# A bias table stored once instead of 128 times, two norm borders with their filler products moved, and two matrix products padded with zero rows

## The chip, the core and the metric

The kernel runs on one core of one Trainium2 chip, as one launch. A core has four compute engines that matter here: TensorE (PE, matrix products, with its weight loads shown apart as PEld), VectorE (DVE), ScalarE (ACT) and GpSimd (POOL); SyncE (SP) issues the DMA transfers of this kernel, all on one queue that 16 DMA engines work off. Each engine runs its own instructions in program order and waits on semaphores for the others. The metric is the device time of one execution in microseconds (us), the median of several runs.

## What is computed

A chain of three transformer-like blocks on one sequence of 256 tokens of width 1024, in float32. Cut to what the change touches:

```
# block 1: retention + RG-LRU, gated (g_l = x_n @ w_in[gl]); rms_norm out
# block 2: attention with relative bias, conv, pooling, then two layer norms
rel  = r[:, None] - r[None, :]                      # query - key, 256 x 256
own  = q @ k.T * 64**-0.5 + tab[t5_bucket(rel)]     # tab: rel_bias, 8 heads x 32 buckets
own  = where(rel >= 0, own, -1e30)
attn = softmax(own) @ v
x = layer_norm(alpha * x + mix, ln1_g, ln1_b)       # border 1
up = causal_dwconv(x @ w_up, ffn_conv_w) + ffn_conv_b
x = layer_norm(alpha * x + (u * silu(g)) @ w_down, ln2_g, ln2_b)   # border 2
# block 3: swiglu_ffn(rms_norm(x)), rwkv7 time mix, swiglu, cross attention to a memory
#          (k, v = rms_norm(mem) @ w), gmlp
kk = kk / max(norm(kk, per head), 1e-12)            # rwkv: 16 heads of 64
g  = sigmoid(xg @ g1) @ g2                          # rwkv gate, inner width 160
```

## The kernel before

**Tiling.** Activations lie feature-major: x is [128 partitions, 8, 256 tokens]. All weights stream through SBUF as blocks of 1 MB (128 x 2048 float32). `_dma` (L434) issues one block on SP; `_split` then cuts each half of it into two parts, a rounded high half that ACT copies (L455) and the low remainder that DVE subtracts (L458). A product is three passes over those parts in PE (L543/L547 for 512 and 256 wide operands, L545 to L547, L562 to L564 for token-major output), accumulated in PSUM tiles `psd` (4 buffers) and `psx` (4 buffers).

**Order.** The order of instructions on each engine is that in which the Python code emits them. Evictions and side work are put off by `later`, `soon` and `chain`: closures that `tick` and `tock` run at each later column group. `pump` issues the next weight block and the next splits when an estimate of the DMA queue (`_queued(us)`, a clock that each transfer advances) says they fit.

**Bias table.** `bias_table` (L1205 to L1221) multiplies a one-hot bucket matrix (33 x 384, from `_buckets`) with the bias values (33 x 8): L1217 on PE, L1218 copies the 8 x 384 result out on ACT, and L1219 writes it to DRAM, each head's row 128 times (8 x 128 x 384 float32, 1.57 MB). This is emitted in block 1, between blocks of the weights `w_in_k` and `w_in_gl`. Block 2 reads it back at L1230 as a tile of 128 x 8 x 256, in which each partition starts one element earlier in its own copy of the row, and `top()` adds it to the scores (L1264, shown in the trace under L369, the helper that issues it).

**Borders.** `ln_finish` (L1081 to L1130) is the layer norm after a linear layer; it runs after the attention output (border 1, into `up`) and after `down` (border 2, into the first ffn of block 3). In it PE has the mean product (L1089, which needs the accumulated `acc` of L1079), then the variance product (L1104), and DVE the subtraction (L1093), the reciprocal root (from L374 on) and the normalised outputs (L369). Since PE would have nothing else, `fill(n)` puts n memory units there: each is 16 matmuls of the memory's keys (L543/L547) or values (L566/L567), with an eviction later (L628/L629, or at the values a scaled one, L366/L369). The argument `units` says how many stand ahead of the mean product, between it and the variance product, and behind. At border 2 the norm factor of the next rms norm follows: `rms_stats(nxt, at)` emits L721 and its DVE steps from L724 on, `at` calls of `tick` later, inside the first column group of the ffn.

**Rwkv.** L1805 multiplies the per-head factors `nt` (8 rows) with `heads` (8 rows) and L1839 the second part of the gate (32 rows of 160), both with the contraction on 8 or 32 partitions.

Of the kernel before, what the change touches and what calls it, by code (L numbers as in the profile page):

```python
# [10 lines left out]
F32 = mybir.dt.float32  # L11
# [7 lines left out]
P = 128  # L19
T = 256  # L20
# [95 lines left out]
def _buckets():  # L116

    n = np.arange(T)
    nf = np.maximum(n, 1).astype(np.float32)
    large = 16 + (np.log(nf / np.float32(16)) / np.float32(math.log(64)) * np.float32(16)).astype(np.int32)  # L120
    bucket = np.where(n < 16, n, np.minimum(large, 31))
    out = np.zeros((33, 384), np.float32)
    for i in range(384):
        rel = 255 - i
        out[bucket[rel] if rel >= 0 else 32, i] = 1.0
    return out

# [174 lines left out]
class Net:  # L302
# [775 lines left out]
        elif m > 1:  # L1078
            self.nc.vector.tensor_add(st["acc"], st["acc"], xm)  # L1079

    def ln_finish(self, st, gname, bname, nxt=None, units=(1, 2, 3)):  # L1081

        nc, x = self.nc, self.x
        if nxt is None:
            xp = Pair(self, KD)
        self.keep = 2
        late = self.fill(units[0])
        ps = self.psum("x")
        nc.tensor.matmul(ps[:, :T], self.mean, st["acc"], start=True, stop=True)  # L1089
        sq = {}  # L1090
        for k in range(KD + 2):
            if k < KD:
                nc.vector.tensor_sub(x[:, k], x[:, k], ps[:, :T])  # L1093
                sq[k] = self.tmp("t")
                self.act(sq[k], x[:, k], AF.Square)
            if k > 2 and k % 2:
                self.stt(sq[k - 3], sq[k - 3], 1e-5 * 2 * D / P / KD, sq[k - 2], ALU.add, ALU.add)
        late += self.fill(units[1])
        self.pump()
        self.pump()  # L1100
        self._rest()
        ps = self.psum("x")
        for k in range(0, KD, 2):
            nc.tensor.matmul(ps[:, :T], self.mean, sq[k], start=k == 0, stop=k == KD - 2)  # L1104
        for f in late:
            f()
        r = self.tmp("rB", bufs=2)
        self.rsqrt(r, ps[:, :T], self.tmp("na", bufs=1))
        late = self.fill(units[2])
        ts = {}  # L1110
        for k in range(KD + 1):
            if k < KD:
                t = ts[k] = self.tmp("t")
                self.stt(t, x[:, k], self.col(gname, k), r, ALU.mult, ALU.mult)
                self.act(x[:, k], t, bias=self.col(bname, k))
                if nxt is None:
                    self.act(xp.hi(k), t, bias=self.col(bname, k))
                else:
                    self.rms_feed(nxt, k, x[:, k])
            if k and nxt is None:  # L1120
                self.stt(xp.lo(k - 1), ts[k - 1], self.col(bname, k - 1), xp.hi(k - 1).bitcast(F32), ALU.add, ALU.subtract)
            elif k:
                self.tick()
            if k == 3:
                for f in late:
                    f()
        self.drain()
        if nxt is None:
            return xp
        self.rms_stats(nxt, at=1)  # L1130

    def mem_start(self):

# [72 lines left out]
    def bias_table(self):  # L1206

        nc, io = self.nc, self.io
        oh = self.tmp("e", 512, bufs=4)[:33, :392]
        nc.sync.dma_start(oh[:, :384], io["bucket"])  # L1210
        nc.sync.dma_start(oh[:, 384:], io["relb"])
        row = self.tmp("e", 512, bufs=4)[:8, :384]
        self.bias_dram = self.pd.tile([8, P, 384], F32, name="bias_dram", tag="bias_dram")

        def run():
            ps = self.psum("x")
            nc.tensor.matmul(ps[:8, :384], oh[:, 384:], oh[:, :384], start=True, stop=True)  # L1217
            nc.scalar.copy(row, ps[:8, :384])  # L1218
            nc.sync.dma_start(self.bias_dram, row[:, None].to_broadcast([8, P, 384]))  # L1219
            self._queued(4.4)  # L1220
        self.later(6, run)  # L1221

    def block2(self, st):

        nc, io, x = self.nc, self.io, self.x
        mul, add = ALU.mult, ALU.add
        xp, r = st["xp"], st["r"]
        bias = self.slot([P, 8, T])
        b = self.bias_dram
        nc.sync.dma_start(bias, bass.AP(tensor=b.tensor, offset=b.offset + 127, ap=[[383, P], [P * 384, 8], [1, T]]))  # L1230
        misc = self.slot([P, 7 * T + 2 * P])
        pool = misc[:, 5 * T:]
        nc.sync.dma_start(pool, io["pool"])
# [12 lines left out]
        v, at = vat[:, :2], vat[:, 2:]  # L1246
# [7 lines left out]
        def soft(h):  # L1254
            s = slice(64 * (h % 2), 64 * (h % 2) + 64)
            ps = self.psum("x")
            nc.tensor.matmul(ps[:, :P], q[s, h // 2, :P], k_[s, h // 2, :P], start=True, stop=True)
            nc.tensor.matmul(ps[:, P:384], q[s, h // 2, P:], k_[s, h // 2], start=True, stop=True)
            e = es[:, h % 5]
            parts = ((0, slice(0, P)), (1, slice(P, 384)))  # L1260

            def top():
                for t, s in parts:
                    self.stt(e[:, s], ps[:, s], 0.125, bias[:, h, P - t * P:], mul, add)  # L1264
                    nc.vector.tensor_reduce(mx[:, h, t:t + 1], e[:, s], AX.X, ALU.max)
                self.ts(mx[:, h], mx[:, h], -1.0)

            def expo():
                for t, s in parts:
                    self.act(e[:, s], e[:, s], AF.Exp, bias=mx[:, h, t:t + 1], accum_out=S[:, h, t:t + 1])  # L1270
            self.soon(top)
            self.chain(expo, lambda: turn(h, e))

        def turn(h, e):
            nc.vector.reciprocal(S[:, h], S[:, h])
            pt = self.psum("x")
            for a in range(3):
                nc.tensor.transpose(pt[:, a * P:(a + 1) * P], e[:, a * P:(a + 1) * P], self.ident)
            self.soon(lambda: nc.scalar.copy(e[:, :384], pt[:, :384]))
            self.later(1 + max(0, 2 - h), lambda: attend(h, e))  # L1280
# [85 lines left out]
        st = {"acc": self.tmp("acc", bufs=2)}  # L1366
# [30 lines left out]
        st = {"acc": self.tmp("acc", bufs=2)}  # L1397
# [4 lines left out]
        nxt = self.rms_start("ffn1_norm_3", want="cols")  # L1402
# [210 lines left out]
    def rwkv(self, st, nxt):  # L1613
# [5 lines left out]
        nc, io, x, r = self.nc, self.io, self.x, st["r"]  # L1619
        mm, mul, add = nc.tensor.matmul, ALU.mult, ALU.add  # L1620
# [3 lines left out]
        self.done()  # L1624
        cst = self.slot([P, 1218 + 2 * T])
        nc.sync.dma_start(cst[:, :1218], io["rwc"])
        nt = cst[:8, 1218:].rearrange("p (f t) -> p f t", f=2)
        sel, reset = cst[:, :2], cst[:, 2:258]
        lev = cst[:, 258:386].rearrange("p (b c) -> p b c", b=4)
        nlev1, id32 = cst[:, 386:418], cst[:, 418:450]  # L1630
        gmask = cst[:, 450:706].rearrange("p (e c) -> p e c", e=2)
        heads = cst[:8, 706:1218].rearrange("p (j c) -> p j c", j=4)
        wl = [self.slot([P, WB]) for _ in range(3)]
        for t, n in zip(wl, ("lora1", "lora2", "lora3")):
            nc.sync.dma_start(t[:, :io[n].shape[1]], io[n])
        h, dx = self.slot([P, KD, T]), self.slot([P, KD, T])
# [69 lines left out]
        psl, sums = [], []  # L1706
        lt = wl[2][:, :576].rearrange("p (s c) -> p s c", s=2)
        tw = wl[2][:, 1280:].rearrange("p (n t) -> p n t", n=3)

        def lora(k):  # L1710
            if k == 0:
                psl.extend(self.psum("x") for _ in range(2))
            for n, (t, w, c) in enumerate(zip(ts.pop(k), (c1[:, k, :64], c1[:, k, 64:], g1[:, k]), (0, 64, P))):
                for s in range(2):
                    mm(psl[s][:, c:c + w.shape[1]], t[:, s * P:(s + 1) * P], w, start=k == n == 0, stop=k == 7,
                       skip_group_check=True)
            if k == 7:
                squash()
# [52 lines left out]
        def turn_norms(f):  # L1771
            ps = self.psum("x")
            for s in range(2):
                nc.tensor.transpose(ps[:8, s * P:(s + 1) * P], nn[:, 1, s, 8 * f:8 * f + 8], self.ident)
            self.soon(lambda: nc.scalar.copy(nt[:, f], ps[:8, :T]))
        self.later(5, lambda: norms(0), post=True)
        self.later(9, lambda: norms(1), post=True)

# [54 lines left out]
        def gates(m):  # L1833

            ps = self.psum("x")
            for i in range(2):
                s, o = slice((m + i) * P, (m + i + 1) * P), ps[:, i * T:(i + 1) * T]
                mm(o, wl[1][:, s], tw[:, 1], start=True, stop=False)
                mm(o, wl[1][:32, 1024 + (m + i) * P:1024 + (m + i + 1) * P], tw[:32, 2], start=False, stop=True)  # L1839
            nc.scalar.copy(flat(g[:, m:m + 2]), ps)  # L1840


# [288 lines left out]
        for m in range(0, 8, 2):  # L2131
            gates(m)
# [157 lines left out]
```

## Time and profile before

| what | value |
|---|---|
| three runs | 1838.8, 1840.44, 1840.64 us, median 1840.44 |
| the profiled execution's own time | 1836.93 us |
| its span | 1835.0 us |
| PE busy | 1784.6 us, 97% of the span |
| DVE busy | 1257.4 us, 69% |
| ACT busy | 914.0 us, 50% |
| POOL busy | 13.2 us, 1% |
| mean granted TensorE clock | 0.987 |
| DMA, mean over the span | 170 GB/s, 311.90 MB |

The span runs from the first to the last instruction that the profiler shows; 1.93 us of the execution lie around it. The profiled execution was 3.5 us shorter than the median of the runs. A granted clock of 1.00 is TensorE's upper level (2.4 GHz) and 0.50 its lower one (1.2 GHz); a stretch with both shows a value between.

### The profile page before, as it was taken

To read this page: it belongs to the slowest core of one execution; us is meant where nothing else is said; L and a number is where in the kernel's file an instruction comes from. 1 tells how busy PE (TensorE), PEld (TensorE's weight loads), DVE (VectorE), ACT (ScalarE), POOL (GpSimd) and SP (SyncE) were. 2 spreads that over 40 slices of the span, in tenths; PEclk is the share of its full clock that TensorE was granted. 3 is DMA by queue.
4 is the path that set the end of the run, shared out by engine and by line. 5 is a ranking of instruction groups with operands and counts; after the bars stand their busy time and mean duration, and the time that the engine had idled before them with its cause. 6 is when DMAs were issued, how large, how long until landed. Compare 5 with 4: busy or idle time off the path is not lost.

```text
span 1835.0 us, 27642 instructions
## 1 busy us (share of the span) xinstructions
PE 1784.6 (97%) x11142; PEld 1555.9 (85%) x11142; DVE 1257.4 (69%) x2300; ACT 914.0 (50%) x1550; POOL 13.2 (1%) x31
## 2 busy tenths in 40 slices
PE   9969999999998999999989999999999999999997
PEld 8859889899987888888589888888888899888886
DVE  7858777898757655578677675556556578676553
ACT  7738646476535544253224454444444555454441
POOL 0000000000000000001000000000000000000000
PEclk9979999999999999999989999999999999999999
DMA  8455544454563545532324354455445635445450
GB/s 312 142 147 207 186 168 167 155 188 178 186 214 130 200 171 203 184 120 78 98 103 187 135 207 172 149 201 213 162 159 207 250 118 210 159 169 194 163 184 23
DMA packets 56511, 311.90 MB, mean 170 GB/s; under 512 B 13727, under 2 KB 17856, under 8 KB 20160
## 3 DMA queue, kind: packets, MB, share of 16 engines
q1 hardware_dynamic: 56384, 310.15, 46.8%
q8 instruction: 87, 1.43, 0.3%
q14 instruction: 40, 0.33, 0.1%
HBM read 304.36 MB, written 5.77 MB: 169 GB/s over the span
## 4 chain that ended last, share of the span: by engine, by line
PE 89%; DVE 5%; DMA 3%; ACT 2%; issue 1%; SPq 0%; DVEq 0%; ACTq 0%
PE psd L543 17%; PE psd L547 14%; PE psd L562 10%; PE psd L564 10%; PE psd L563 10%; PE psd L545 5%; PE psd L546 5%; DMA s<-w_in_gl 2%; PE psx L543 2%; PE psd L2168 1%; PE psd L557 1%; DVE s L458 1%; PE psd L540 1%; PE psx L1452 1%; PE psx L547 1%
## 5 line engine op out<-in xcount | busy, mean ns | idle before, releaser
L458 DVE TENSOR_TENSOR s<-s,s 128x1024 fp32r<-128x1024 f32 x524 | 627.3, 1221 | 198.2 <-ACT s L455 197.7
L547 PE MATMUL psd<-s,s 128*128 128x256 f32 x2336 | 658.9, 282 | 3.0 <-DVE s L458 2.8
L455 ACT CAST s<-s 128x1024 fp32r<-128x1024 f32 x524 | 532.4, 1046 | 201.7 <-PE psd L547 100.6
L543 PE MATMUL psd<-s,s 128*128 128x512 f32 x1392 | 495.2, 399 | 0.0
L547 PEld LDWEIGHTS psd<-s,s 128*128 128x128 f32 x2336 | 445.1, 191 | 4.9 <-DVE s L458 4.3
L562 PE MATMUL psd<-s,s 128*128 128x512 f32 x816 | 324.9, 398 | 1.9 <-DVE s L369 1.9
L564 PE MATMUL psd<-s,s 128*128 128x512 f32 x816 | 319.6, 392 | 0.0
L563 PE MATMUL psd<-s,s 128*128 128x512 f32 x816 | 319.0, 391 | 0.0
L543 PEld LDWEIGHTS psd<-s,s 128*128 128x128 f32 x1392 | 262.1, 188 | 63.3
L545 PE MATMUL psd<-s,s 128*128 128x256 f32 x944 | 272.8, 289 | 18.6 <-DVE s L960 18.2
L546 PE MATMUL psd<-s,s 128*128 128x256 f32 x944 | 268.0, 284 | 0.0
L545 PEld LDWEIGHTS psd<-s,s 128*128 128x128 f32 x944 | 181.9, 193 | 20.5 <-DVE s L960 18.4
L546 PEld LDWEIGHTS psd<-s,s 128*128 128x128 f32 x944 | 182.0, 193 | 0.1
L562 PEld LDWEIGHTS psd<-s,s 128*128 128x128 f32 x816 | 153.9, 189 | 33.2 <-DVE s L369 2.3
L564 PEld LDWEIGHTS psd<-s,s 128*128 128x128 f32 x816 | 153.9, 189 | 33.1
L563 PEld LDWEIGHTS psd<-s,s 128*128 128x128 f32 x816 | 154.1, 189 | 30.6
L1456 DVE TENSOR_TENSOR s<-psx,s 128x512 fp32r<-128x512 f32 x44 | 30.4, 692 | 95.5 <-ACT s L1458 80.0
L366 ACT ACTIVATE t<-psd,rc 128x256 f32<-128x256 f32 x88 | 41.6, 475 | 103.5 <-PE psd L564 103.3
L1458 ACT CAST s<-psx 128x512 fp32r<-128x512 f32 x40 | 23.5, 587 | 122.4 <-PE psx L1452 122.4
L369 DVE SCALAR_TENSOR_TENSOR t<-psd,rc,t 128x256 f32<-128x256 f32 x88 | 41.5, 482 | 47.5 <-ACT t L366 47.5
L366 ACT ACTIVATE t<-x 128x256 f32<-128x256 f32 x86 | 34.1, 407 | 66.8 <-DVE x L369 45.5
L366 ACT ACTIVATE s<-x,vecs 128x256 fp32r<-128x256 f32 (+1 forms) x80 | 40.2, 506 | 50.0 <-DVE x L1416 36.4
(380 smaller groups left out, 1846.3 us busy)
## 6 DMA issues: line engine op xcount, KB each, us to landing
s<-w_ffn_in SPq DMA_DIRECT2D x88, 1024.0 KB, 4.8
s<-w_ffn_out SPq DMA_DIRECT2D x44, 1024.0 KB, 4.8
s<-w_up SPq DMA_DIRECT2D x22, 1024.0 KB, 4.9
s<-w_out SPq DMA_DIRECT2D x12, 1024.0 KB, 4.9
s<-w_down SPq DMA_DIRECT2D x11, 1024.0 KB, 4.7
s<-w_xq SPq DMA_DIRECT2D x8, 1024.0 KB, 4.8
s<-w_xo SPq DMA_DIRECT2D x8, 1024.0 KB, 4.9
s<-w_gm_v SPq DMA_DIRECT2D x8, 1024.0 KB, 4.8
```

The costliest lines, as they stand in the source:

```text
L366: return self.nc.scalar.activation(out, in_, func, **kw)
L369: return self.nc.vector.scalar_tensor_tensor(out, in0, scalar, in1, op0=op0, op1=op1)
L455: self.nc.scalar.copy(hi, raw[:, s])
L458: self.nc.vector.tensor_sub(lo, raw[:, s], hi.bitcast(F32))
L543: mm(out, w[0], x.two(k), start=first, stop=False)
L545: mm(out[:, :T], w[0], x.hi(k), start=first, stop=False)
L546: mm(out[:, :T], w[0], x.lo(k), start=False, stop=False)
L547: mm(out[:, :T], w[1], x.hi(k), start=False, stop=last)
L562: mm(out, hi, w[0], start=first, stop=False)
L563: mm(out, hi, w[1], start=False, stop=False)
L564: mm(out, lo, w[0], start=False, stop=last)
L1456: rest = lambda: nc.vector.tensor_sub(lo, both, hi.bitcast(F32))
```

## The change

Three edits that don't touch one another.

- The table in DRAM is 8 x 384, written once (12 KB instead of 1.57 MB), and the estimate of the queue no longer advances for it. `_buckets` runs the other way, and the read at L1230 takes, for partition p, 256 elements from offset p + 1 of each row, in ascending order; `top()` walks them backwards (`[::-1]`).
- `ln_finish` has `units=(2, 2, 2)` instead of `(1, 2, 3)`, and `rms_stats` is called with `at=3` instead of 1.
- In the rwkv part `nt` and `heads` use all 128 partitions and the gate product L1839 too; POOL sets `nt` (128 x 512) and a third of `tw` (128 x 256) to zero first, two MEMSETs more.

```
 _buckets:
-        rel = 255 - i
+        rel = i - P
 ln_finish:
-    def ln_finish(self, st, gname, bname, nxt=None, units=(1, 2, 3)):
+    def ln_finish(self, st, gname, bname, nxt=None, units=(2, 2, 2)):
-        self.rms_stats(nxt, at=1)
+        self.rms_stats(nxt, at=3)
 bias_table:
-        self.bias_dram = self.pd.tile([8, P, 384], F32, name="bias_dram", tag="bias_dram")
+        self.bias_dram = self.pd.tile([8, 384], F32, name="bias_dram", tag="bias_dram")
-            nc.sync.dma_start(self.bias_dram, row[:, None].to_broadcast([8, P, 384]))
-            self._queued(4.4)
+            nc.sync.dma_start(self.bias_dram, row)
 block2:
-        nc.sync.dma_start(bias, bass.AP(tensor=b.tensor, offset=b.offset + 127, ap=[[383, P], [P * 384, 8], [1, T]]))
+        nc.sync.dma_start(bias, bass.AP(tensor=b.tensor, offset=b.offset + 1, ap=[[1, P], [384, 8], [1, T]]))
-                    self.stt(e[:, s], ps[:, s], 0.125, bias[:, h, P - t * P:], mul, add)
+                    self.stt(e[:, s], ps[:, s], 0.125, bias[:, h, :P + t * P][:, ::-1], mul, add)
 rwkv:
-        nt = cst[:8, 1218:].rearrange("p (f t) -> p f t", f=2)
+        nt = cst[:, 1218:].rearrange("p (f t) -> p f t", f=2)
-        heads = cst[:8, 706:1218].rearrange("p (j c) -> p j c", j=4)
+        heads = cst[:, 706:1218].rearrange("p (j c) -> p j c", j=4)
+        nc.gpsimd.memset(nt, 0.0)
+        nc.gpsimd.memset(tw[:, 2], 0.0)
-            self.soon(lambda: nc.scalar.copy(nt[:, f], ps[:8, :T]))
+            self.soon(lambda: nc.scalar.copy(nt[:8, f], ps[:8, :T]))
-                mm(o, wl[1][:32, 1024 + (m + i) * P:1024 + (m + i + 1) * P], tw[:32, 2], start=False, stop=True)
+                mm(o, wl[1][:, 1024 + (m + i) * P:1024 + (m + i + 1) * P], tw[:, 2], start=False, stop=True)
```

On SP the order of all transfers stays; only the size of the one row at L1219 differs. PE at border 1, before: the last pair of the one memory unit that stands ahead of the mean product L1089 (`acc_410` is the sum, `psd_` the units' PSUM tiles, `s18` and `s7` weight halves), and the first pair behind it.

```order
L543 MATMUL psd_439_3543<-s18_264_2083,s16_423_3448 128x512
L547 MATMUL psd_439_3543<-s18_264_2083,s16_423_3448 128x256
L1089 MATMUL psx_441_3561<-acc_410_3334,misc_8_104 128x256
L543 MATMUL psd_450_3591<-s7_263_2082,s11_424_3451 128x512
L547 MATMUL psd_450_3591<-s7_263_2082,s11_424_3451 128x256
```

The same place after, from the last pair of the same unit (`psd_439`) on:

```order
L543 MATMUL psd_439_3543<-s18_264_2083,s16_423_3448 128x512
L547 MATMUL psd_439_3543<-s18_264_2083,s16_423_3448 128x256
L543 MATMUL psd_441_3561<-s7_263_2082,s11_424_3451 128x512
L547 MATMUL psd_441_3561<-s7_263_2082,s11_424_3451 128x256
...
L543 MATMUL psd_441_3561<-s18_264_2083,s11_424_3451 128x512
L547 MATMUL psd_441_3561<-s18_264_2083,s11_424_3451 128x256
L1089 MATMUL psx_442_3578<-acc_410_3334,misc_8_104 128x256
L543 MATMUL psd_451_3608<-s7_263_2082,s10_427_3476 128x512
```

A second unit of 16 matmuls (`psd_441`) now stands ahead of L1089; at border 2 one unit moves in the same way, and at both borders two instead of three stand behind the variance product.

PE at border 2, before: the place of the norm factor's product L721 in the first column group of the ffn (`psd_721` and `psd_722` are the two token halves, `s17` the split activations of row block k, `s15` and `s4` weight halves).

```order
L564 MATMUL psd_722_6025<-s15_674_5759,s17_677_5785 128x512
L721 MATMUL psx_724_6040<-misc_8_104,acc_676_5784 128x1 x2
L562 MATMUL psd_721_6024<-s4_675_5777,s17_677_5785 128x512
L563 MATMUL psd_721_6024<-s4_675_5777,s17_677_5785 128x512
L564 MATMUL psd_721_6024<-s4_675_5777,s17_677_5785 128x512
```

After:

```order
L564 MATMUL psd_722_6025<-s20_695_5890,s8_678_5786 128x512
L721 MATMUL psx_727_6072<-misc_8_104,acc_676_5784 128x1 x2
L562 MATMUL psd_721_6024<-s1_696_5892,s8_678_5786 128x512
L563 MATMUL psd_721_6024<-s1_696_5892,s8_678_5786 128x512
L564 MATMUL psd_721_6024<-s1_696_5892,s8_678_5786 128x512
```

L721 has moved from behind 12 matmuls of the group (row blocks k = 0 and 1) to behind 36 (k = 0 to 5), out of 48. On DVE the steps that follow it stood behind one weight split before:

```order
L704 TENSOR_TENSOR acc_676_5784<-acc_676_5784,t_717_6014 128x256
L458 TENSOR_TENSOR s5_723_6038<-s10_680_5804,s5_723_6038 128x1024
L724 COPY rcv_719_6022<-psx_724_6040 128x2
L374 TENSOR_SCALAR rc_718_6021<-rcv_719_6022 128x2
L671 TENSOR_TENSOR rca_720_6023<-rc_718_6021 128x2
```

and stand behind three after:

```order
L704 TENSOR_TENSOR acc_676_5784<-acc_676_5784,t_717_6014 128x256
L458 TENSOR_TENSOR s5_723_6038<-s10_680_5804,s5_723_6038 128x1024
L458 TENSOR_TENSOR s3_724_6052<-s10_680_5804,s3_724_6052 128x1024
L458 TENSOR_TENSOR s12_726_6069<-s0_681_5806,s12_726_6069 128x1024
L724 COPY rcv_719_6022<-psx_727_6072 128x2
```

So two splits that were behind the norm factor are now ahead of it on DVE.

## Rows read from the trace of the kernel before

**Rows 1.** PE's waits over the whole span: waiting line, releaser, total us, times, longest.
```profile
PE psd L545 <- DVE s L960: 18.2, 1, 18.2
PE psx L1937 <- issue: 3.9, 1, 3.9
```

**Rows 2.** SP's issues around the table's write: start us, us, instruction, count.
```profile
88.08 0.83 SPq L1219 DMA_DIRECT2D bias_dram<-e  x1
89.02 19.30 SPq L434 DMA_DIRECT2D s<-w_in_gl  x3
```

**Rows 3.** Windows: us, busy of five engines (count), granted clock, DMA share, GB/s.
```profile
90.00:100.00 10.00, 10.00 (x86) 10.00 (x85) 9.38 (x18) 6.82 (x11) 0.00 (x0) 1.00 0.46 51
...
128.00:133.00 5.00, 4.91 (x23) 4.91 (x24) 4.90 (x12) 3.37 (x7) 0.00 (x0) 0.50 0.78 298
133.00:138.00 5.00, 5.00 (x40) 4.89 (x40) 4.93 (x13) 3.45 (x11) 0.00 (x0) 0.97 0.08 31
```

**Rows 4.** DMA issues by tensor: count, KB each, median us from issue to landing.
```profile
s<-w_in_gr SPq DMA_DIRECT2D x4, 1024.0 KB, 4.7
...
s<-bias_dram SPq DMA_DIRECT2D x1, 1024.0 KB, 5.5
```

**Rows 5.** ACT's timeline at the stall; brackets hold idle time before and releaser.
```profile
124.02 1.99 ACT L455 CAST s<-s 128x1024 fp32r<-128x1024 f32 x2 [20.96 <-DMA s<-w_in_gl]
```

**Rows 6.** DVE's timeline at the stall, and its first use of decay.
```profile
125.10 1.22 DVE L458 TENSOR_TENSOR s<-s,s 128x1024 fp32r<-128x1024 f32 x1 [20.28 <-ACT s L455]
...
133.05 0.41 DVE L988 TENSOR_TENSOR e<-psx,s 128x256 f32<-128x256 f32 x1
```

**Rows 7.** PE's timeline at the stall.
```profile
128.09 0.58 PE L545 MATMUL psd<-s,s 128*128 128x256 f32 x1 [18.25 <-DVE s L960]
```

**Rows 8.** PE's timeline at border 1: the mean product, and the start of up.
```profile
341.16 0.91 PE L1089 MATMUL psx<-acc,misc 128*128 128x256 f32 x2 [3.61 <-DVE acc L1079]
...
359.04 0.28 PE L545 MATMUL psx<-s,s 128*128 128x256 f32 x1
```

**Rows 9.** DVE's timeline at border 1: the evictions, and the first output's low half.
```profile
349.75 1.08 DVE L629 TENSOR_TENSOR s<-psd,s 128x256 f32<-128x256 f32 x3
...
355.95 0.49 DVE L369 SCALAR_TENSOR_TENSOR s<-t,vecs,s 128x256 fp32r<-128x256 f32 x1 [0.64 <-ACT s L366]
```

**Rows 10.** Windows at the two borders, columns as in rows 3.
```profile
551.40:556.75 5.35, 5.35 (x33) 4.67 (x32) 4.69 (x13) 4.41 (x10) 0.00 (x0) 1.00 0.44 135
577.00:580.40 3.40, 3.40 (x10) 2.66 (x10) 3.12 (x11) 2.57 (x3) 0.00 (x0) 0.51 0.10 41
341.10:345.00 3.90, 3.84 (x12) 3.24 (x13) 2.90 (x10) 2.16 (x6) 0.00 (x0) 0.56 0.18 74
```

**Rows 11.** PE's timeline at border 2, the ffn's first group.
```profile
569.55 0.51 PE L562 MATMUL psd<-s,s 128*128 128x512 f32 x1 [1.89 <-DVE s L369]
...
576.40 0.61 PE L721 MATMUL psx<-misc,acc 128*128 128x1 f32 x4 [3.16 <-DVE acc L704]
...
586.49 0.39 PE L564 MATMUL psd<-s,s 128*128 128x512 f32 x1
```

**Rows 12.** DVE's timeline at border 2: the first output's low half, the last sum.
```profile
565.14 0.48 DVE L369 SCALAR_TENSOR_TENSOR s<-x,vecs,s 128x256 fp32r<-128x256 f32 x1 [0.65 <-ACT s L366]
...
575.92 0.42 DVE L704 TENSOR_TENSOR acc<-acc,t 128x256 f32<-128x256 f32 x1
```

**Rows 13.** PE's groups in the rwkv part, by shape: count, busy us, mean ns.
```profile
L1838 PE MATMUL psx<-s,s 128*128 128x256 f32 x16 | 5.6, 431 | 0.0
...
L1839 PE MATMUL psx<-s,s 32*128 32x256 f32 x16 | 5.6, 426 | 0.0
```

**Rows 14.** SP's issue of the table's read.
```profile
227.66 0.39 SPq L1230 DMA_DIRECT2D s<-bias_dram  x1
```

**Rows 15.** DVE's first use of the table.
```profile
260.70 0.28 DVE L369 SCALAR_TENSOR_TENSOR s<-psx,s 128x128 f32<-128x128 f32 x1
```

**Rows 16.** Window behind PE's wait at L1937, columns as in rows 3.
```profile
921.80:932.00 10.20, 7.91 (x113) 7.54 (x114) 6.21 (x13) 1.12 (x3) 0.00 (x0) 0.50 0.47 173
```

## The prediction, made before the changed kernel ran

> **What bounds the kernel now.** I read the page's totals first: TensorE (PE) is busy 97% of the span, so an edit pays only where PE waits, or runs at its lower clock. PE's list of waits came next. One wait of 18.2 us leads it, then 3.9 us at L1937 [rows 1]; the mean product of border 1 (3.61 us) and the norm factor's product of border 2 (3.16 us) follow [rows 8, 11]. The three edits point at three of these four places. For each I then read the timelines around it, to see what ends the wait, and the windows, to see the granted clock. Everywhere else PE runs back to back, and work taken from other engines there is worth nothing.
>
> The long wait has a simple cause. PE waits for VectorE (DVE), which waits 20.28 us for a cast on ScalarE (ACT), which waits 20.96 us for the first block of `w_in_gl` [rows 5 to 7]. That block was issued at 89.02, right behind the table's write at 88.08 [rows 2], and was there at 124.02: 35.0 us, where the same kind of block otherwise takes 4.7 [rows 4]. Between 90 and 100 us the queue moved only 51 GB/s with 0.46 of the engines' time [rows 3]. The write's 1.57 MB at that rate take 31 us, which covers 88 to 119; the block behind it needs the rest.
>
> **The table's write.** Removed: 1.57 MB on the queue. Added: 12 KB in its place, in the same order. The first block, issued at about 89, then lands near 94 and the two behind it near 99 and 104, at 4.7 us each and one after another. DVE's restart at 125.10 moves to where it stopped, 104.8, which is 20.28 earlier. PE gains its 18.25. It also gains clock: 23 matmuls from 128 to 133 ran at 0.50, where 40 fit in the next five us [rows 3]; at the upper level those 23 take 2.9 instead of 4.9 us, so 2.0 more, 20.3 in all, which is also what DVE can give. What is late next is `decay`, queued behind the three blocks. DVE first uses it 7.95 us after its restart (133.05 - 125.10) [rows 6], so at 112.8. If SP issues it no earlier than before (89.02 + 19.30 = 108.3) it lands at 113.0 and costs 0.2; the three blocks no longer hold SP so long, so I take 0. DVE, not PE, then sets the pace of the stretch, with casts and splits following the blocks. **Term A: 20.3 us**, between 17 (another 3 us of waiting for blocks) and 21.
>
> The read at L1230 moves as much as before, 1,024 rows of 1 KB, but from a region of 12 KB. It is issued at 227.66 [rows 14] and first used at 260.70 [rows 15]; landing took 5.5 [rows 4], so it has 27.5 us of cover. At the worst rate of these rows, 51 GB/s, 1.05 MB take 20.6 us: still hidden, so 0. The backward walk adds no operation on DVE; L369 took 0.28 us for 128 columns [rows 15]. From nothing to twice that (16 such operations, at most 0.42 us each: 6.7 us spread over the attention) it stays on DVE, beside PE. I take 0.
>
> **Border 1.** A unit is 16 matmuls; 33 took 5.35 us at full clock [rows 10], so 2.7 us a unit. The unit moved ahead of L1089 fills most of the 3.61 us wait [rows 8]; 0.9 is left. What starts `up` is then not PE but DVE: the first low half is done at 355.95 + 0.49 = 356.44 [rows 9], while `up` began at 359.04 [rows 8], when PE had finished three units behind the variance product. With two behind it, PE has to wait a little for a PSUM buffer, since four units now stand before the evictions at 349.75 [rows 9], and then about 1 us for the low half. One more eviction (1.08 / 3 = 0.36) ahead of the reciprocal root and an L1089 that no longer runs at the lower clock (0.91 us [rows 8]) about cancel. **Term B1: 359.04 - 356.44 = 2.6**, from 0 (the wait only moves) to 4.4 (the wait and the loss of the slow stretch both go).
>
> **Border 2.** Here L1089 did not wait, so the moved unit delays the mean product, and with it DVE's chain, by 2.7 us plus one scaled eviction (0.4): about 3 us. The first low half comes at 565.62 + 3.1 = 568.7, the last sum at 576.34 + 3.0 = 579.3 [rows 12]. PE's own work in front of the ffn is the same, six units, to 566.8, so it now waits 1.9 us for the first low half; before, it waited 1.89 us a little later [rows 11]. But then it has 36 matmuls in front of L721 instead of 12. A pair of 512 and 256 columns takes 0.33 us (5.35 for 33 matmuls [rows 10]), so one of 512 about 0.22 and the six of a row block k 1.35. Blocks 0 to 2 end at 572.8. The eight low halves and sums fill DVE from 568.7 to 579.3, 1.3 us each, with two evictions among them ahead of the fourth, so block 3 waits about 1 us for its half; block 5 ends near 577.8, L721 waits 1.5 us for the sum, and blocks 6 and 7 end at 579.3 + 0.6 + 2.7 = 582.6. Before, the group ended at 586.49 + 0.23 = 586.7 [rows 11]. **Term B2: 4.1, taken as 4.0**, from -1 (the 3 us of DVE reach PE and the clock falls as before) to 5.5.
>
> The norm factor itself comes later: behind L721 DVE has three splits of 1.22 us [rows 6] instead of one, so it starts at 579.3 + 0.6 + 3.7 = 583.6 and is ready about a microsecond later. The first group's eviction on ACT waits for it. Two groups fit the four PSUM buffers, and the second, 48 matmuls of 0.22 us, keeps PE busy until 593: hidden, and without that cover it would cost 2 us.
>
> **The padded rows.** A product over 32 rows took 426 ns, over 128 rows 431 [rows 13]. 32 changed products times 5 ns is 0.2 us at most; I take 0. The two MEMSETs and the copies that wait for them stand on an engine that is busy 1% of the span, and nothing is queued behind them that PE needs soon.
>
> **Sum.** 20.3 + 2.6 + 4.0 = 26.9 us. The profiled execution took 1836.93 (a span of 1835.0 and 1.93 around it) and would take 1810.0. It was 3.5 us below the median of the runs, 1840.44, and I put the sum against that: **1813.5**.
>
> **Rivals.**
> *R1, the clock still falls at the borders.* Stretches at half clock stand behind the waits of both: 0.56 for 3.9 us, 0.51 for 3.4 us [rows 10], each losing 1.7 us. The shorter waits speak against it, their number (three at border 2) for it. One fall at each: 26.9 - 3.4 = 23.5, giving 1816.9.
> *R2, the borders only move their waits.* PE waits for the same DVE chain in other places, B1 and B2 are nothing: 1820.1.
> *R3, the padded rows lift a slow stretch.* From 921.8 to 932 the clock is at its lower level, with PE busy 7.91 us [rows 16]; at the upper level that work would take 4 us less: 1809.5. It lies 6 us behind the gate products, but behind PE's wait of 3.9 us too [rows 1], which the padding leaves. The Trainium skill (TensorE: Matmul & The Clock Gate, "Part 1: The HAM clock gate") has the clock follow how busy the engine has been and names no rows; by it R3 gives nothing.
> *R4, slower: the read from one small region.* All partitions now read the same twelve KB. If that crowds one place of the memory, the price is the landing time beyond the 33.0 us from 227.66 to 260.70, one for one, as PE waits for the scores. The gain is used up at 33 + 26.9 = 60 us, that is under 17.5 GB/s; at 10 GB/s the read takes 105 us and the kernel 1840.4 - 26.9 + 72 = 1885.5. The slowest rate in these rows is 51, so it needs a third of that. The Trainium skill (DMA: Bandwidth & Descriptors, "Latency and other measured facts") has a row for copies whose rows fall onto the same places by their pitch: 207 GB/s drop to 103. An estimate by that page is twice 5.5 us, 11 us, still hidden; no row of before shows such a read.
> *R5, the write is not what holds the block.* If something else keeps the first block until 124 (SP's order, a semaphore), A is nothing and the gain is 6.6: 1833.8. The low rate of rows 3 ahead of it speaks against that.
>
> **How the numbers follow.** The forecast has 0.55 (its own range 1811 to 1816), R1 0.22, R2 0.10, R3 0.06, R4 0.03, R5 0.04. The range goes from 1809 (R3) to 1821 (R2, and the forecast with A at 17 at either clock) and leaves out R4, R5 and the tails, 0.15. About 0.2% (3.7 us) is what a measurement of this kernel can tell from no change; all but R4 lie beyond that on the faster side. Faster 0.96, same 0.01, slower 0.03.
>
> **What would show it.** A: no wait over 2 us at L545 before 130 us, the blocks of `w_in_gl` landing in about 5 to 10 us, the clock at 1.00 from 105 to 138. B1: the wait at L1089 near 1 us and `up` starting about 2.6 us sooner after it. B2: L721 behind 36 matmuls with a wait under 2 us, and the first group's end 4 us sooner. Padding: L1805 and L1839 at 426 to 431 ns. R4: a landing at L1230 above 33 us. The prediction is wrong if PE waits for `decay` or for a later block in place of the first, or if the half-clock stretches stand where they stood.

## The result, and the profile after

The changed kernel takes **1808.78 us** (median of 4 runs, 1807.12 to 1811.4) against 1840.54 us before (also 4 runs): a ratio of 0.9825, with a 95% interval of 0.9805 to 0.9846. The gain is 31.8 us where 26.9 was forecast. The sign, the table's term and the borders' sum were right; the time lies 0.2 us below the forecast's range (1809 to 1821) and 4.7 us below the forecast itself (1813.5).

The page's first lines of the changed kernel: the span, and busy time by engine.

```profile
span 1805.4 us, 27651 instructions
PE 1776.4 (98%) x11142; PEld 1552.9 (86%) x11142; DVE 1256.9 (70%) x2300; ACT 914.0 (51%) x1550; POOL 13.4 (1%) x33
```

PE's waits after, in the columns of rows 1:

```profile
PE psx L1938 <- issue: 3.4, 1, 3.4
...
PE psx L721 <- DVE acc L704: 1.4, 1, 1.4
...
PE psd L543 <- DVE s L629: 0.9, 1, 0.9
...
PE psx L1089 <- DVE acc L1079: 0.8, 1, 0.8
PE psd L564 <- DVE s L369: 0.7, 1, 0.7
PE psd L562 <- ACT s L366: 0.7, 1, 0.7
```

The 18.2 us of [rows 1] are gone, 3.61 has become 0.8 and 3.16 has become 1.4. What remains on top is the 3.4 us at L1938 (L1937 before), a line that no edit touches.

**The stall.** SP's issues around the table's write, after; then two windows with the columns of rows 3:

```profile
87.60 0.30 SPq L1219 DMA_DIRECT2D bias_dram<-e  x1
87.98 11.10 SPq L434 DMA_DIRECT2D s<-w_in_gl  x3
99.18 0.39 SPq L976 DMA_DIRECT2D s<-decay  x1
```

```profile
105.00:110.00 5.00, 5.00 (x41) 4.89 (x40) 4.90 (x11) 1.64 (x6) 0.00 (x0) 1.00 0.20 54
...
120.00:130.00 10.00, 10.00 (x83) 9.83 (x82) 7.60 (x21) 8.30 (x30) 0.00 (x0) 1.00 0.53 202
```

The three blocks now keep SP 11.1 us instead of 19.3 [rows 2], `decay` is issued at 99.18 and not at 108.3, and PE is busy in both windows at the upper clock, where before it waited 18.25 us and then ran at half clock [rows 3, 7]. From block issue to landing the table of DMA issues says 5.1 us for `w_in_gl`, 6.9 for `decay`, and 5.3 for the read of the small table, against 5.5 in [rows 4]:

```profile
s<-w_in_gl SPq DMA_DIRECT2D x4, 1024.0 KB, 5.1
...
s<-decay SPq DMA_DIRECT2D x1, 1024.0 KB, 6.9
s<-bias_dram SPq DMA_DIRECT2D x1, 1024.0 KB, 5.3
```

**The borders.** PE's timeline after, border 1 and then border 2, answering to [rows 8, 11]:

```profile
320.11 0.70 PE L1089 MATMUL psx<-acc,misc 128*128 128x256 f32 x2 [0.78 <-DVE acc L1079]
...
328.97 0.50 PE L543 MATMUL psd<-s,s 128*128 128x512 f32 x1 [0.88 <-DVE s L629]
...
335.03 0.38 PE L545 MATMUL psx<-s,s 128*128 128x256 f32 x1
...
544.88 0.50 PE L562 MATMUL psd<-s,s 128*128 128x512 f32 x1 [0.66 <-ACT s L366]
...
550.46 0.50 PE L564 MATMUL psd<-s,s 128*128 128x512 f32 x1 [0.70 <-DVE s L369]
...
555.75 0.61 PE L721 MATMUL psx<-misc,acc 128*128 128x1 f32 x4 [1.37 <-DVE acc L704]
...
558.84 0.39 PE L564 MATMUL psd<-s,s 128*128 128x512 f32 x1
```

The waits are where the forecast put them: 0.78 us at L1089, 0.88 for a PSUM buffer, and about 0.4 between the first products of `up` at border 1; at border 2 one at the first block (0.66 us, where 1.9 was forecast), one at a later one (0.70, forecast about 1), and 1.37 at L721 (forecast 1.5).

**Where the rest came from.** Comparing start times of the same products in the two traces gives how far the changed kernel is ahead at each place: 21.0 to 21.3 us behind the stall (0.5 of it from the first 35 us, where no edit lies), 23.5 behind border 1, 27.3 at the first product that needs the ffn's evicted first group (L1452 before, L1451 after: 592.16 and 564.84), 28.1 at 800 us of the kernel before, 26.4 at 811, 27.7 at the first gate product (906.51 and 878.85) and 30.5 at the last one (915.91 and 885.43). The 1.7 us between 800 and 811 went by a fall of the clock to its lower level, at 780 to 783 us of the changed kernel. So about 4 us come from the rwkv part, and 2.8 of them within the ten us of the gate products. That is the padding, which the forecast had at nothing.

### The profile page after: what moved, and what is told of

Read it like the earlier page. It is cut to its first block, busy times and chain, and to the rows that moved or that the text cites. A ratio compares the mean times of both kernels' runs of the same rounds, so it can differ in the third digit from the quotient of the medians.

```text
span 1805.4 us, 27651 instructions
## 1 busy us (share of the span) xinstructions
PE 1776.4 (98%) x11142; PEld 1552.9 (86%) x11142; DVE 1256.9 (70%) x2300; ACT 914.0 (51%) x1550; POOL 13.4 (1%) x33
## 4 chain that ended last, share of the span: by engine, by line
PE 89%; DVE 7%; ACT 2%; issue 1%; DMA 1%; SPq 0%; DVEq 0%; ACTq 0%
PE psd L543 17%; PE psd L547 14%; PE psd L562 10%; PE psd L564 10%; PE psd L563 10%; PE psd L545 5%; PE psd L546 5%; DVE s L458 2%; PE psx L543 2%; PE psd L2169 2%; PE psd L557 1%; PE psd L540 1%; PE psx L1451 1%; PE psx L547 1%; ACT s L366 1%
## 5 line engine op out<-in xcount | busy, mean ns | idle before, releaser
L563 PEld LDWEIGHTS psd<-s,s 128*128 128x128 f32 x816 | 153.4, 188 | 30.5
L1457 ACT CAST s<-psx 128x512 fp32r<-128x512 f32 x40 | 23.5, 587 | 120.7 <-PE psx L1451 120.7
```

The costliest lines, as they stand in the source:

```text
L563: mm(out, hi, w[1], start=False, stop=False)
```

## The experiments

Each is an edit of the kernel before or of the changed kernel, timed beside the kernel before on the same chip. The medians of before were 1839.46, 1838.98 and 1839.12 us in the three sets.

**The table alone.** The edit is the five lines of `_buckets`, `bias_table`, `block2` and `top()` in the diff above.

> The kernel before with the table's edit alone: written once, read backwards. Theory (three edits that add up, the stall being the bytes of the write on the queue): 20.6 us less than before, the waits at L545 and the half-clock stretch behind it gone, both borders and the gate products as before. Rival (the gains depend on each other: with the stall gone the borders already run differently): 23 us or more. Rival (the stall is not the write's): under 3 us.

Measured: 1818.91 us, ratio 0.9894 (0.9878 to 0.991), 20.55 us less (16.6 to 22.4 by the interval). Neither rival fits; the term stands as it was forecast, 20.3.

**Half the copies.** Does the stall follow the bytes of the write?

```
-        self.bias_dram = self.pd.tile([8, P, 384], F32, name="bias_dram", tag="bias_dram")
+        self.bias_dram = self.pd.tile([8, 64, 384], F32, name="bias_dram", tag="bias_dram")
-            nc.sync.dma_start(self.bias_dram, row[:, None].to_broadcast([8, P, 384]))
+            nc.sync.dma_start(self.bias_dram, row[:, None].to_broadcast([8, 64, 384]))
-        nc.sync.dma_start(bias, bass.AP(tensor=b.tensor, offset=b.offset + 127, ap=[[383, P], [P * 384, 8], [1, T]]))
+        for c in range(2):
+            nc.sync.dma_start(bias[64 * c:64 * c + 64], bass.AP(tensor=b.tensor, offset=b.offset + 127 - 64 * c,
+                                                               ap=[[383, 64], [64 * 384, 8], [1, T]]))
```

> The kernel before with 64 copies of each row instead of 128 (0.79 MB written), read by two transfers of 64 partitions. Theory (the stall is the bytes of the write on the queue, at the 50 GB/s of the trace): the first block of w_in_gl lands 15 us sooner, the wait at L545 is 18.2 - 15.5 = 3 us, and with the shorter half-clock stretch the kernel takes 16 to 18 us less. Rival (the stall comes from the write standing ahead of the blocks at all, or from SP): wait of 18 us as before.

Measured: 1824.05 us, ratio 0.9919 (0.9906 to 0.9933), 14.9 less. PE's wait, and the block's time from issue to landing, in this kernel's trace:

```profile
PE psd L545 <- DVE s L960: 2.5, 1, 2.5
...
DMA to landing us min/median/max: 19.2/19.2/19.2
```

Landing fell from 35.0 to 19.2 us, that is by 15.8 for 0.79 MB less, 50 GB/s; the wait fell from 18.2 to 2.5. The packets of the two traces show the write itself: 1,024 of 1,536 bytes, from 89.5 to 121.2 us, in the kernel before, and 512 of them, from 89.7 to 105.6, here. So the stall follows the size of the write at about 50 GB/s, and not its mere place in the queue. Packets and bytes were halved together, so the runs don't tell which of the two sets the rate. The time came down by a little less than the 16 to 18 expected, which the interval (12.3 to 17.3) still touches.

**The borders alone.**

```
-    def ln_finish(self, st, gname, bname, nxt=None, units=(1, 2, 3)):
+    def ln_finish(self, st, gname, bname, nxt=None, units=(2, 2, 2)):
-        self.rms_stats(nxt, at=1)
+        self.rms_stats(nxt, at=3)
```

> The kernel before with units (2, 2, 2) and the norm factor at 3 alone. Theory: 6.5 us less (3.0 at border 1, 3.5 at border 2), the wait of 18.2 us stays. Rival (the borders give nothing, the missing gain lies elsewhere): within 1 us. Rival (all that the sum of the prediction missed lies here): 10 us.

Measured: 1830.63 us, ratio 0.9958 (0.9945 to 0.997), 8.8 less. The interval is 5.5 to 10.1 us: it shuts out the first rival, but holds the theory's 6.5 and the second rival's 10. The trace decides between these two: by the starts of the same products this kernel is 2.5 us ahead of the kernel before behind border 1, 5.9 behind border 2, 7.1 at 775 us and 5.9 at the end. So the borders gave about what was forecast, and what the sum missed does not lie there.

**The norm factor's place alone.** Only `at=1` becomes `at=3`; the units stay.

> The kernel before with the norm factor moved behind 36 instead of 12 matmuls alone; the units stay (1, 2, 3). Theory (at border 2 the gain comes from the norm factor's place, and the moved unit only costs DVE 3 us there): the wait of 3.2 us at L721 is gone, 3 to 5 us less than before, border 1 unchanged. Rival (the unit is what helps at border 2, by keeping the clock up): under 1.5 us.

Measured: 1832.0 us, ratio 0.996 (0.9945 to 0.9975), 7.1 less. More than expected, and here is why. PE's timeline at border 2 and a window at border 1 of this kernel:

```profile
569.57 0.50 PE L562 MATMUL psd<-s,s 128*128 128x512 f32 x1 [1.88 <-DVE s L369]
...
577.17 0.50 PE L721 MATMUL psx<-misc,acc 128*128 128x1 f32 x4
...
341.00:345.00 4.00, 2.96 (x16) 2.58 (x17) 3.14 (x10) 1.52 (x5) 0.00 (x0) 1.00 0.41 172
```

L721 no longer waits: 36 matmuls cover DVE's chain completely when that chain starts without the extra unit ahead of it. The first group ends at 580.4 against 586.7 before, 6.3 us sooner. Only 3.2 us of this is the wait: the clock stayed at its upper level through the group, though the buffer wait of 1.88 us is the same as in [rows 11], behind which it fell in the kernel before (570.2 to 573.6 us, and again 577.0 to 580.4). At border 1, which this edit doesn't touch, it stayed up too, and that gave 0.9 us more.

**The changed kernel with the old units at border 2.**

```
-        self.ln_finish(st, "ln2_g_2", "ln2_b_2", nxt)
+        self.ln_finish(st, "ln2_g_2", "ln2_b_2", nxt, units=(1, 2, 3))
```

> The changed kernel with units (1, 2, 3) at border 2 alone; border 1 keeps (2, 2, 2). Theory (as above): L721 waits no more, since DVE's chain starts 2.7 us sooner, and the wait for a PSUM buffer of 1.9 us is back at the first group; 0 to 2.5 us less than the changed kernel. Rival (the buffer wait pulls the clock down as before): 1 to 2 us more.

Measured: 1805.48 us (1804.21 to 1807.88), ratio 0.9818 (0.9801 to 0.9835). The changed kernel itself, run again in the same set:

> The changed kernel unaltered, beside the next three on one chip. Theory (table 20.5, borders 6.5, padding 4): 31 us less than before. Rival (the 31.8 us of the first result hold some luck of the clock): 28 to 29.

Measured: 1808.27 us (1806.7 to 1811.78), ratio 0.9835 (0.9817 to 0.9854), 30.85 less than before. So the first result repeats, and the version with (1, 2, 3) at border 2 is 2.8 us faster by the medians, although in its profiled execution L721 no longer waits and the clock fell behind the 1.9 us buffer wait:

```profile
546.50 0.50 PE L562 MATMUL psd<-s,s 128*128 128x512 f32 x1 [1.89 <-DVE s L369]
...
545.00:550.00 5.00, 3.50 (x11) 2.72 (x12) 4.00 (x11) 3.94 (x11) 0.00 (x0) 0.77 0.00 0
```

The two intervals overlap, so 2.8 is likely rather than shown. The traces agree with it where the clock was alike. What border 2 gave, by the starts of the same products from behind border 1 to 806 us, was 6.3 us with (1, 2, 3) in the kernel before with only the norm factor moved and 4.7 with (2, 2, 2) in the changed kernel run again, both with no fall of the clock there; with one fall each it was 4.7 with (1, 2, 3) here and 2.5 with (2, 2, 2) in the changed kernel without the padding (below). By these four traces the old units are about 2 us better at border 2, and one fall of the clock takes that away. It is the fastest version measured here by its median.

**The norm factor later still.** In the changed kernel, `at=3` becomes `at=4`, behind all 48 matmuls of the group.

> The changed kernel with the norm factor at 4, behind all 48 matmuls of the first group. Theory (what is left at L721 is a wait for the sum): the wait of 1.4 us goes, the factor comes later but two groups fit the PSUM buffers; 1 to 1.4 us less than the changed kernel. Rival (the later factor holds up the first group's eviction and PE waits for a buffer): 0 to 2 us more.

Measured: 1809.79 us, ratio 0.9838 (0.9821 to 0.9855), 1.5 more than the changed kernel beside it, well inside the spread. The trace shows why nothing was gained: the wait at L721 is gone, and one of 2.9 us stands at L1451, which needs the evicted first group.

```profile
PE psx L1451 <- DVE t L369: 2.9, 1, 2.9
...
562.95 0.16 DVE L369 SCALAR_TENSOR_TENSOR rc<-rca,rc 128x2 f32<-128x2 f32 x1
...
563.21 0.84 ACT L366 ACTIVATE t<-psd,rc 128x256 f32<-128x256 f32 x2 [3.55 <-DVE rc L369]
```

So the trace bears the rival out, with another waiter than it named: not a buffer but a product inside the second group's work. At `at=3` that consumer waits 0.2 us.

**The padded rows alone.** The edit is the rwkv part of the diff.

> The kernel before with the zero-padded rows alone. Theory (a product over 32 rows between two over 128 keeps the weights of each from being loaded beside the product ahead of it, 0.19 us at each change of the row count): 3.0 to 3.5 us less, L1839 and L1838 start 0.43 us apart by pairs instead of 0.63. Rival (the prediction's own: rows change nothing): within 0.3 us. Rival (the padding lifts the clock behind it): the half-clock stretch behind L1937 shrinks and the pairs stay 0.63 apart.

Measured: 1835.5 us, ratio 0.9978 (0.9969 to 0.9987), 4.0 less. In the trace 2.9 us of this come at the gate products. The clock behind them did not improve; this window of the padded kernel holds the half-clock stretch of [rows 16] still, and its granted clock is 0.62, where the same window of the kernel before has 0.72:

```profile
916.00:934.00 18.00, 14.44 (x292) 13.88 (x292) 13.41 (x28) 2.86 (x8) 0.00 (x0) 0.62 0.62 251
```

**The changed kernel without the padding.**

> The changed kernel without the padded rows (table and borders alone). Theory: 3.0 to 3.5 us more than the changed kernel's time, so 27 to 28 us less than before, which is the prediction's sum of 26.9. Rival (the padding gives nothing): the changed kernel's time within 0.5 us.

Measured: 1813.12 us, ratio 0.9853 (0.9837 to 0.9869), 26.3 less than before, with runs from 1809.7 to 1819.57. The forecast's sum was 26.9 and its time 1813.5.

**The gate alone.** Of the padding, only `tw` and L1839.

> The kernel before with the gate product's rows padded alone (32 to 128); nt and heads stay at 8 rows. Theory (each change of the row count between neighbours costs 0.19 us, because the next weights aren't loaded beside the product ahead): the 15 changes among the 16 gate products go, 15 x 0.195 = 2.9 us less than before. Rival (the heads products carry the padding's gain): under 1 us.

Measured: 1835.5 us, ratio 0.998 (0.9971 to 0.999), 3.5 less. The gate carries most of it; what the heads' products add, half a microsecond here, is less than the runs can tell apart. The traces can: between 811 and 870 us, where the heads' products lie, the kernel with all the padding gains 1.2 us and this one nothing; at the gate products both gain 2.9.

**Why: the row count, or its change?** Two kernels tell these apart. The first leaves the 32 rows and turns the order around in every second output:

```
-                mm(o, wl[1][:, s], tw[:, 1], start=True, stop=False)
-                mm(o, wl[1][:32, 1024 + (m + i) * P:1024 + (m + i + 1) * P], tw[:32, 2], start=False, stop=True)
+                two = [(wl[1][:, s], tw[:, 1]), (wl[1][:32, 1024 + (m + i) * P:1024 + (m + i + 1) * P], tw[:32, 2])]
+                for n, (l, r) in enumerate(two[::-1] if i else two):
+                    mm(o, l, r, start=n == 0, stop=n == 1)
```

> The kernel before with 32 rows as they are, but in every second gate output the 32-row product stands ahead of the 128-row one, so that neighbours have the same row count at every second place (128, 32, 32, 128, 128, ...). Theory (it is the change of the row count): 7 of the 15 changes go, 7 x 0.195 = 1.4 us less; in the trace the starts inside a pair of equal row counts are 0.43 us apart, those across a change 0.63. Rival (a product over 32 rows is itself slower to start, whatever its neighbour): no gain, 0.63 us at every 32-row product.

Measured: 1837.61 us, ratio 0.9992 (0.9983 to 1.0001), 1.4 less, as expected, but no difference at all still lies inside the interval. In the trace 1.4 us come at the gate products, and the weight loads (PEld) of this kernel show where: start, busy us, count, and the idle time ahead of the group.

```profile
908.13 0.72 PEld L1840 LDWEIGHTS psx<-s,s 32*128 32x128 f32 x4 [0.33 <-issue]
909.19 0.73 PEld L1840 LDWEIGHTS psx<-s,s 128*128 128x128 f32 x4 [0.33 <-issue]
910.25 0.72 PEld L1840 LDWEIGHTS psx<-s,s 32*128 32x128 f32 x4 [0.33 <-issue]
```

Two neighbours of equal row count now form one group with one idle time of 0.33 us ahead of it, 1.06 us a group. Before, every product had its own, 0.63 us each:

```profile
908.39 0.29 PEld L1839 LDWEIGHTS psx<-s,s 32*128 32x128 f32 x2 [0.33 <-issue]
909.01 0.30 PEld L1838 LDWEIGHTS psx<-s,s 128*128 128x128 f32 x2 [0.33 <-issue]
```

1.06 is 0.63 + 0.43, so a 32-row product behind a 32-row one costs what a 128-row one behind a 128-row one does.

The second pads to 64 rows instead of 128:

```
-                mm(o, wl[1][:32, 1024 + (m + i) * P:1024 + (m + i + 1) * P], tw[:32, 2], start=False, stop=True)
+                mm(o, wl[1][:64, 1024 + (m + i) * P:1024 + (m + i + 1) * P], tw[:64, 2], start=False, stop=True)
```

> The kernel before with the gate product padded to 64 rows instead of 128. Theory (any change of the row count costs): no gain, starts stay 0.63 us apart. Rival (only a product over a quarter of the rows costs, half would do): 2.9 us less, starts 0.43 us apart. Rival (the cost goes with the rows that are missing): between, about 0.5 us apart.

Measured: 1839.46 us, ratio 1.0002 (0.9993 to 1.0012), no gain. PE's starts:

```profile
909.08 0.70 PE L1840 MATMUL psx<-s,s 64*128 64x256 f32 x2
909.71 0.70 PE L1839 MATMUL psx<-s,s 128*128 128x256 f32 x2
910.34 0.70 PE L1840 MATMUL psx<-s,s 64*128 64x256 f32 x2
```

0.63 us apart, as with 32 rows in the kernel before:

```profile
908.39 0.69 PE L1839 MATMUL psx<-s,s 32*128 32x256 f32 x2
909.01 0.70 PE L1838 MATMUL psx<-s,s 128*128 128x256 f32 x2
```

So the change of the row count costs the same for 128 and 32 as for 128 and 64. In the changed kernel the same starts are 0.43 apart, and the weight loads have no idle time ahead of them:

```profile
880.25 0.59 PE L1840 MATMUL psx<-s,s 128*128 128x256 f32 x2
880.68 0.59 PE L1839 MATMUL psx<-s,s 128*128 128x256 f32 x2
...
880.03 0.41 PEld L1840 LDWEIGHTS psx<-s,s 128*128 128x128 f32 x2
880.47 0.41 PEld L1839 LDWEIGHTS psx<-s,s 128*128 128x128 f32 x2
```

The price at each change is 0.33 us without a weight load and 0.195 us (0.627 - 0.432) of PE's time. The Trainium skill (TensorEngine Tiling (Array Packing), "Key Properties") says that changing the tiling mode drains TensorE; its list of modes ("Available Configurations") has 128, 64 or 32 rows. These traces fit that if a product over fewer rows counts as such a mode, which no run here shows.

## Why the prediction was right, and where it was wrong

- **The table's write (20.3 forecast).** Right in mechanism and size: 20.55 alone, and the traces are 20.6 us apart from 35 us to the end of the stall's stretch. `decay` was not late, because SP was free 9 us sooner. Half the copies took 15.8 us off the landing, 50 GB/s where the forecast read 51 from [rows 3].
- **The read and the backward walk (0).** Right: landing 5.3 us, so R4 has nothing. DVE's first use took 0.29 us after and 0.28 in [rows 15], and the eight uses of 128 columns have a mean of 290 ns in both traces.
- **Border 1 (2.6).** Right in the trace: from the first unit's end to the start of `up` it was 21.5 us before (337.55 to 359.04) and is 18.5 now (316.5 to 335.03), 3.0 less, of which about 0.5 goes again at the next products' waits: 2.5 behind the border.
- **Border 2 (4.0).** The sum was right: from L1089 to the first group's end 35.95 us before, and 28.98 + 2.75 for the moved unit now, 4.2 less. Its parts were opposed: the norm factor's place gives 6.3 in the trace where it was tried alone, about half of it by a clock that stayed up, and the moved unit takes about 2 of that back by delaying DVE. The forecast saw that delay (3 us on DVE's chain), but not that the edit without it would probably be better. Its separate waits were less exact than their sum (0.66 us at the first block for 1.9).
- **R1 (the clock falls again).** In the two profiled executions of the changed kernel it did not fall at either border. That is not a property of the edit alone: without the padding, with the same borders and the same 1.4 us wait at L721, it fell (0.50 from 559.6 to 563.0 us), and behind the same 3.6 us wait at L1089 it was 0.56 in [rows 10] and 1.00 in the kernel with only the norm factor moved.
- **The padded rows (0): the step that failed.** It compared how long one product lasts, 426 and 431 ns [rows 13], and took the difference, 0.2 us over 32 products, as the cost. But the two stand in turn in the stream, so each has a change of the row count ahead of it and both carried the cost. In the changed kernel, where both have 128 rows, they last 386 and 379 ns (the lines are one further down there), and the forecast's own sign, 426 to 431 ns, did not come:

```profile
L1839 PE MATMUL psx<-s,s 128*128 128x256 f32 x16 | 4.9, 386 | 0.0
L1840 PE MATMUL psx<-s,s 128*128 128x256 f32 x16 | 4.8, 379 | 0.0
```

  The whole price is in the starts. They were 0.627 us apart at every change between 32 and 128 rows and 0.432 without one, and that was to be read in the trace of before, where the list of PEld's waits has it:

```profile
PEld psx L1839 <- issue: 2.7, 8, 0.3
PEld psx L1838 <- issue: 2.0, 6, 0.3
PEld psx L1751 <- issue: 1.9, 6, 0.3
PEld psx L1805 <- issue: 1.3, 4, 0.3
```

  PE's own list of waits shows none of it, since a matmul there counts as busy until the next; the forecast's premise that PE runs back to back outside of its waits fell with that. The 15 changes among the gate products are 15 x 0.195 = 2.9 us, and the heads' products, eight over 8 rows, 1.2 (26.4 ahead at 811, 27.7 ahead of the gate): 4.1 in the trace, 4.0 in the run of the padding alone. R3 named the padding for a gain of 4.0, but by way of the clock, which did not change: the size was right by accident.
- **The rest.** Without the padding the kernel took 1813.12 us, beside 1813.5 forecast. So the 4.7 us between forecast and result are the padding's 4.0 and 0.7 that the runs' spread covers. The range's lower end stood on R3 alone and had no term for the cost of changing rows.

What stays open: the borders alone gave 8.8 us and the sum of the single edits (20.55 + 8.8 + 4.0 = 33.35) is 2.5 more than all three together (30.85; 31.8 in the first set). The runs of one kernel spread by 3 to 10 us, and the longer ones have the lower granted clock: the changed kernel run again took 1806.7 us at 0.995 and 1811.78 at 0.991. A fall of the clock comes in some executions and not in others (780 to 783 us in one of the two traces of the changed kernel, at 1.7 us), so this difference was not resolved.

## What to carry to other kernels

Where PE has no waits left, read the distance between starts, and the waits of the weight loads, not the length of a matmul. A product over fewer rows between full ones cost 0.195 us at both its borders here; padding it with zeros to the full rows took that away, and ordering equal row counts next to each other did so at every second place. A transfer that repeats data for the reader's convenience costs its bytes on the queue, and it is the next block that pays; store it once and let the access pattern do the repeating. When filler work is moved ahead of a step to cover one wait, look at who else starts from that step: at border 2 the filler delayed DVE and, by the traces, took back about 2 of the 6.3 us that the other edit gave.

## What the runs showed of the hardware that was not expected

- A change of the row count between neighbouring matmuls (128 and 32, or 128 and 64) kept PE from loading the next weights beside the running product: 0.33 us without a load, whichever of the two came first, and 0.627 us between starts for 0.432. Between equal neighbours, 32 or 128 rows, there was no such gap.
- The write of 1,024 rows of 1,536 bytes from 8 partitions went at 50 GB/s with 0.46 of the DMA engines' time, while the blocks of 1 MB that stood behind it landed in about 5 us once it was gone. Halving it halved its time (packets over 31.7 us, then over 15.9).
- A walk backwards over the second operand cost VectorE nothing: eight operations of 128 columns took 290 ns in the mean either way.
- The same wait of PE was followed by the lower clock in one execution and not in another: 3.61 us at L1089 with 0.56 behind it, 3.60 with 1.00.
